# Two-layer hybrid encoder trunk: the low half of every second weight slab made by ScalarE and an adding transfer

## The chip, the core and the metric

The kernel runs on one core of a Trainium2 chip, as one program. Time is device microseconds (us) of one execution. TensorE (PE) multiplies matrices, VectorE (DVE) and ScalarE (ACT) work element by element, GpSimd (POOL) does some element work and issues some transfers, and SyncE (SP) only issues transfers between DRAM and the on-chip memory. Each engine takes its instructions strictly in the order in which they stand in its queue; engines wait for each other through semaphores.

## The reference

512 tokens with 1024 features pass through two layers. Each layer adds a normed mixer and a normed feed-forward block (FFN) to the stream x:

```python
for i in range(DEPTH):                       # two layers
    h = _rmsnorm(x, norm_g[i, 0])
    if i % 2 == 0:
        h = _ssd_mlstm_mixer(h, ...)         # one input projection, 16 SSD heads, 8 mLSTM heads, W_out
    else:
        h = _gla_mixer(h, ...)               # projections, 4 gated-linear-attention heads, W_out
    x = x + _rmsnorm(h, norm_g[i, 1])
    f = _conv_ffn(_rmsnorm(x, norm_g[i, 2]), ...)
    x = x + _rmsnorm(f, norm_g[i, 3])

def _conv_ffn(h, w_up, conv_w, conv_b, w_down):
    u = _dwconv(h @ w_up, conv_w, conv_b)
    gate, val = jnp.split(u, 2, axis=-1)
    return (jax.nn.gelu(gate, approximate=True) * val) @ w_down
```

All of it is in float32. Nearly all arithmetic is the products with the weights: 234 slabs of 128 x 1024 numbers (512 KB each), laid out in DRAM in the order in which they are used (`in_w`).

## The kernel before

**A float32 product in three faster ones.** PE multiplies the type fp32r faster than float32, but rounds its operands. So each operand is kept as two parts: `hi`, its copy rounded to fp32r, and `lo`, what the rounding took off (`lo = raw - hi`). `mm3` adds three products for each 128x128 tile of weights: hi x hi, hi x lo of the activations, and lo x hi. The `lo` slab is thus read by the third matmul of each tile.

**The weight stream.** `w_load` has SP load slab i into one of 3 `raw` buffers. `w_prep` makes the two parts: ACT copies `raw` into `hi` (the row "CAST hi<-raw"), DVE subtracts `hi` from `raw` into `lo` ("TENSOR_TENSOR lo<-raw,hi"). There are 5 buffers for `hi` and 5 for `lo` (`W_SPLIT = 5`). `w_take` prepares slabs until 4 beyond the one in use are ready (`W_AHEAD = 4`). As there are 5 buffers, the copy of slab i+4 can begin only when PE has read slab i-1 for the last time.

**Jobs.** A `Job` is one 128-row tile of W^T h: 8 tiles of weights (one slab) by 3 matmuls of 512 columns. `nat_job` takes two slabs at once and gives 256 columns with the tokens on the partitions. In the FFN the jobs follow each other one slab at a time (the down projection takes 11 tiles a job). `run_group` and `run_last` treat the tokens in two halves (RA, RB) where a norm lies between two products: the last four jobs of a block first run for RA, then for RB, so that the norm of RA can go on beside RB. There four slabs or more are held for both halves, and the next ones come late.

**The mixers.** `bal.weave` interleaves the projection jobs with the scans, in which DVE and ACT do most of the work and POOL some additions. Layer 0's mixer fills about 40 to 500 us of the trace, its output projection and norms 500 to 560, its FFN 560 to 880, the norms between the layers 880 to 960, layer 1's mixer 960 to 1140, its output projection and norms 1140 to 1200, its FFN from 1200 on.

**The order.** The program does not fix the order on an engine by its text alone: the framework's scheduler lists the instructions by its own estimates of their times, PE's too. Semaphores then hold each instruction until its operands are there.

**Slab numbers.** The trace leaves out the numbers of buffers. The slabs' `hi` and `lo` instructions stand on ACT and DVE in the order 0 to 233, so a row is assigned to its slab by counting, and PE's matmuls by their order in the built program. Layer 0's output projection runs its second half on slabs 64 to 68, layer 1's on 164 to 167; the FFN of layer 1 begins with 168 to 171, and 233 is the last slab.

Of the kernel before, what the change touches and what calls it, by code (L numbers as in the profile page):

```python
# [17 lines left out]
T = 512  # L18
D = 1024
# [10 lines left out]

# columns of the constant block
_C = {}
# [8 lines left out]
class _Balance:  # L41
    """Work issued so far to TensorE and VectorE, in ns, to weave two streams evenly."""

# [3 lines left out]
    def weave(self, streams, done):  # L47
        """streams: (generator, engine whose work it is paced by, total ns of that work, head start in ns).
        The stream least far along goes on, if what it needs is done."""
        st = [{"g": g, "e": e, "n": float(n), "t": -lead / float(n), "need": None} for g, e, n, lead in streams]  # L50
        while st:
            ok = [x for x in st if x["need"] is None or x["need"] in done]
            assert ok, [x["need"] for x in st]
            x = min(ok, key=lambda x: x["t"])
            t0 = getattr(self, x["e"])
            try:
                x["need"] = next(x["g"])
            except StopIteration:
                st.remove(x)
            x["t"] += (getattr(self, x["e"]) - t0) / x["n"]  # L60


class _Life:
    """First and last use of every work tile, in program order, and from that a slot for each."""

# [15 lines left out]
    def plan(self, slots):  # L81
        """The slot that has been free for longest."""
        until, res = [-1] * slots, []
        for a, z in zip(self.first, self.last):
            i = min(range(slots), key=lambda j: until[j])
            assert until[i] < a or until[i] < 0, "too few slots"
            until[i] = z + 1
            res.append(i)
        return res


class _Eng:
    """An engine that notes which tiles its instructions touch and how long they take."""

# [36 lines left out]
def kernel(ctx: ExitStack, tc: tile.TileContext, xin, wst, cst, dsk, gw2, out, life=None, plan=None):  # L131
# [47 lines left out]

# [1 line left out]
    cc = cp.tile([P, NCONST], F32, name="cc")  # L181
# [30 lines left out]

# [1 line left out]
    wstate = {"raw": {}, "next": 0, "ready": [], "unit": 0}  # L214
# [7 lines left out]
    def w_prep():  # L222
        i = wstate["next"]
        if i >= NSLAB:
            return
        wstate["next"] += 1
        if i not in wstate["raw"]:
            w_load(i)
        raw = wstate["raw"].pop(i)
        hi = wp.tile([P, 1024], F32R, tag="hi", name=f"hi{i}", bufs=W_SPLIT)  # L230
        lo = wp.tile([P, 1024], F32R, tag="lo", name=f"lo{i}", bufs=W_SPLIT)
        S.copy(hi, raw)
        V.tensor_tensor(lo, raw, hi, ALU.subtract)
        wstate["ready"].append((hi, lo))

    def w_take(n, width=P):
        """The next n tiles of `width` columns of the stream, as (hi, lo) pairs."""
        res = []
        for _ in range(n):
            c0 = wstate["unit"]  # L240
            i, o = divmod(c0, 1024)
            while len(wstate["ready"]) < i + 1 + W_AHEAD and wstate["next"] < NSLAB:
                w_prep()
            hi, lo = wstate["ready"][i]
            res.append((hi[:, o:o + width], lo[:, o:o + width]))
            wstate["unit"] += width
        return res

    def mm3(o, a, b, first, last):
        """o += a^T b with operands in two exact parts."""  # L250
        (ah, al), (bh, bl) = a, b
        PE.matmul(o, ah, bh, start=first, stop=False)
        PE.matmul(o, ah, bl, start=False, stop=False)
        PE.matmul(o, al, bh, start=False, stop=last)
# [4 lines left out]
    class Job:  # L259
        """One 128-row tile of W^T h."""  # L260

# [37 lines left out]
    def run_group(jobs, r, mid=None, serial=False):  # L299
        """Several jobs together, one k tile after the other (or one job after the other)."""  # L300
        if not serial:
# [42 lines left out]
    def nat_job(h, post, hi=False):  # L344
        """256 columns of h^T W with tokens on the partitions."""
        w = w_take(KD, 256)
# [12 lines left out]

# [1 line left out]
    def col_sum(o, i, acc):  # L361
        """o[tok, 2i + t]: the sum of acc[:, tok] over the partitions, for two tiles of tokens."""
        for t in range(2):
            PE.matmul(o[:, 2 * i + t:2 * i + t + 1], acc[:, t * P:(t + 1) * P], ones[:, 0:1], start=True, stop=True)

    def rstd(v, rs):
        """rs = 1 / sqrt(v / D + eps) for columns v."""
        S.activation(rs, v, AF.Sqrt, bias=eps1, scale=1.0 / D)
        V.reciprocal(rs, rs)

    def spread(o, rs):
        """o[p, tok] = rs[tok] on every partition."""
        for t in range(2):
            PE.matmul(o[:, t * P:(t + 1) * P], rs[:, t:t + 1].broadcast_to((P, P)), ident, start=True, stop=True)

    def split(xk, g, h, n, r):
        """The two exact parts of x * g (the norm's per-token factor is applied to the products)."""
        if h[n] is None:
# [5 lines left out]
    class Scale:  # L384
        """1 / rms of x for every token: as columns [tok, tile] and as a row on all partitions."""

# [28 lines left out]
    class Post:  # L415
        """x += f * g * rstd, fed with f one row tile and one token half at a time."""

# [26 lines left out]
        def finish(self, r, nxt=None):  # L444
            """nxt: (layer, which, h) of the norm that follows."""
            o = ps()
# [10 lines left out]

# [1 line left out]
    def conv(o, sc, wc, b, taps):  # L459
        """Depthwise convolution along the tokens of a PSUM tile, scaled by token, into SBUF."""  # L460
        half = taps // 2
# [54 lines left out]

# [1 line left out]
    def mixer0(h, x_again, sc, chain_of):  # L518
        done = set()
        # small block: dt and gates  # L520
        smallj = {}
# [22 lines left out]

# [1 line left out]
        rows = {}  # L546
# [11 lines left out]
        def gate_rows():  # L558
# [6 lines left out]
            V.reciprocal(d, d)  # L565
            V.tensor_tensor(u, u, d, ALU.mult)           # z = e / (2 + e)
            z2 = st()
            S.activation(z2, u, AF.Square)
            V.tensor_scalar(d, z2, 2.0 / 15, 2.0 / 13, ALU.mult, ALU.add)
            for j in range(5, -1, -1):  # L570
                V.tensor_tensor(d, d, z2, ALU.mult)
                V.tensor_scalar(d, d, 2.0 / (2 * j + 1), None, ALU.add)
            V.tensor_tensor(u, u, d, ALU.mult)           # log1p(exp(-|g|))
            lo64, hi64 = slice(0, 64), slice(64, 128)
# [32 lines left out]
            yield  # L607
            # SSD rows
            cs = st()
# [13 lines left out]
            yield  # L623
            # mLSTM rows
            ig = st()
# [30 lines left out]
            S.activation(q4[hi64], fc[hi64], AF.Exp)  # L656
            # rows to DRAM for broadcasts over the partitions
            G.dma_start(rowd[lo64], cs[lo64])
# [7 lines left out]
            G.dma_start(dskb, dsk.broadcast_to((P, 16)))  # L666
            # columns: [tok, chunk, (quantity of the pair, direction), head]
            for w, tiles in ((16, (q1, q2)), (8, (q3, q4))):
# [10 lines left out]

# [1 line left out]
        zt = [[None] * 2 for _ in range(NCH)]  # L681
# [12 lines left out]

# [1 line left out]
        def b8(ap):  # L696
# [150 lines left out]

# [1 line left out]
        kT, qT = [None] * 8, [None] * 8  # L849
# [143 lines left out]

# [1 line left out]
        part = [None] * KD  # L995
# [45 lines left out]

# [1 line left out]
    def mixer1(h, x_again, sc, chain_of):  # L1043
# [34 lines left out]
        def after(ins, first):  # L1078
            """Issue order only: groups activations by their function table."""
            tc.add_manual_dep(ins.ins, first.ins.name, mybir.DependencyInfo(  # L1080
# [58 lines left out]
        def head(hd, ps):  # L1139
# [7 lines left out]
            for dd in range(2):  # L1147
                bcv = bcs[dd][hd]
                b3 = bcv.rearrange("p (c l) -> p c l", l=64)
                ei = 63 if dd == 0 else 0  # L1150
                # first / second 64 tokens of a block in the order of the scan
                fi, se = (0, 1) if dd == 0 else (1, 0)
# [10 lines left out]
                after(S.activation(ke, ke, AF.Exp, scale=1.0 / 16.0), pin["ln"])  # L1163
                # kc: keys of the first half to its end, of the second half as they are
                kc, q2 = st(), st()
# [18 lines left out]
                yield  # L1184
                # whole-block operands of the states
                d2 = dec.rearrange("p (c u) -> p c u", u=2)
# [84 lines left out]

# [1 line left out]
    def load_x(src):  # L1273
# [8 lines left out]
    def load_first(r):  # L1282
        """Half the tokens of x, two row tiles to a tile."""
        x = [st() for _ in range(KD // 2)]
# [69 lines left out]
W_SPLIT = 5  # L1354
W_AHEAD = 4
BANKS = {"pj": 2, "ps": 3, "pm": 3}
PA = ("pj", "pm", "ps", "ps", "pm", "pj", "pm", "ps")
# [6 lines left out]
def _layout(a):  # L1364
    """Host-side layout: transposed activations, weights in the order of use, packed vectors."""
    f = lambda n: np.asarray(a[n])
# [84 lines left out]
def build(new, arrays):  # L1451
    """The program: traced once to learn how long each tile is in use, then with a slot for each."""
    plan = None
# [25 lines left out]
```

## Time and profile before

| | us |
|---|---|
| median of 3 runs | 1556.7 (1555.45 to 1556.77) |
| span of the profiled execution, first to last instruction | 1554.8 |
| what lies around the span, taken against the median | 1.9 |
| PE busy | 1508.2 (97%) |
| DVE busy | 1032.1 (66%) |
| ACT busy | 730.6 (47%) |
| POOL busy | 142.8 (9%) |

The result lists no time of its own for the profiled execution; its span is 1554.8 us, and 1.9 us is what the median of the runs lies above it. A matmul's row lasts longer than PE's step from one to the next, because matmuls are pipelined: 24 matmuls of 512 columns take 5.56 us in the FFN. The column "PEclk" is the clock that PE was granted, as a share of 2.4 GHz.

### The profile page before, as it was taken

Reading aid. Unit: us, or ns where it says so; the run is one execution under the profiler, and the core shown is the slowest. Engines: PE = TensorE matmul, PEld = TensorE weight load, DVE = VectorE, ACT = ScalarE, POOL = GpSimd, SP = SyncE. Lnnn points to the kernel's source line nnn. Section 1 sums busy time; section 2 is a strip of 40 time slices with the busy share of each in tenths; the row PEclk is TensorE's granted clock in tenths of the full one; section 3 lists DMA queues with packets and bytes.
Section 4 is the critical chain, followed back from the end, with each engine's and each line's share of the span. In section 5 each row is a group of like instructions: output and inputs, shape, how many; then the busy total and the mean of one; then the engine's idle time right before and its main releaser. Section 6 shows DMA issues by size and latency. Waiting matters only on the chain.

```text
span 1554.8 us, 22022 instructions
## 1 busy us (share of the span) xinstructions
PE 1508.2 (97%) x8616; PEld 1300.3 (84%) x8616; DVE 1032.1 (66%) x1703; ACT 730.6 (47%) x1332; POOL 142.8 (9%) x165
## 2 busy tenths in 40 slices
PE   7989999999999999999999999999999999999997
PEld 6879887888987988888888997898899888888887
DVE  6986789967754888623676378737537974267744
ACT  6445545744642664423444356436545543244432
POOL 5020321212100110000000030000003000000000
PEclk9999999999999999999999999999999999999999
DMA  5243243334322322222222132211131322222211
GB/s 186 96 156 96 82 129 102 102 114 140 131 91 79 112 86 104 95 95 95 95 95 99 69 123 103 74 56 55 65 125 69 109 95 95 95 95 95 95 69 54
DMA packets 67303, 152.46 MB, mean 98 GB/s; under 512 B 6256, under 2 KB 32896, under 8 KB 67200
## 3 DMA queue, kind: packets, MB, share of 16 engines
q1 hardware_dynamic: 61984, 145.77, 27.7%
q10 hardware_dynamic: 4752, 4.23, 0.9%
q8 instruction: 67, 1.10, 0.3%
q0 software_dynamic: 464, 1.06, 0.2%
q14 instruction: 36, 0.29, 0.1%
HBM read 146.42 MB, written 4.59 MB: 97 GB/s over the span
## 4 chain that ended last, share of the span: by engine, by line
PE 80%; DVE 11%; ACT 4%; DMA 3%; issue 2%; POOL 0%; SPq 0%; DVEq 0%; ACTq 0%; POOLq 0%
PE pj L105 31%; PE ps L105 25%; PE pm L105 24%; DVE s L105 8%; DMA s<-rowd 2%; ACT s L105 2%; DVE lo L105 2%; DVE t L105 1%; ACT hi L105 1%; ACT L105 0%; DVE pacc L105 0%; DMA raw<-in_w 0%; POOL s L105 0%; ACT msq L105 0%; DVE rd L105 0%
## 5 line engine op out<-in xcount | busy, mean ns | idle before, releaser
L105 DVE TENSOR_TENSOR lo<-raw,hi 128x1024 fp32r<-128x1024 f32 x234 | 291.4, 1249 | 220.5 <-ACT hi L105 220.3
L105 PE MATMUL pj<-s,hi 128*128 128x512 f32 (+1 forms) x1384 | 405.4, 376 | 5.2 <-ACT s L105 5.2
L105 ACT CAST hi<-raw 128x1024 fp32r<-128x1024 f32 x234 | 244.3, 1048 | 241.7 <-PE pj L105 107.7
L105 PE MATMUL pm<-s,hi 128*128 128x512 f32 (+1 forms) x1140 | 309.9, 357 | 8.4 <-ACT s L105 6.8
L105 PE MATMUL ps<-s,hi 128*128 128x512 f32 (+1 forms) x1140 | 307.3, 356 | 0.7 <-DVE t L105 0.7
L105 PEld LDWEIGHTS pj<-s,hi 128*128 128x128 f32 x1384 | 248.7, 189 | 54.6 <-ACT s L105 5.6
L105 PE MATMUL pj<-s,lo 128*128 128x512 f32 (+1 forms) x692 | 257.3, 372 | 0.0
L105 PE MATMUL pj<-hi,s 128*128 128x256 f32 x1280 | 241.6, 286 | 6.6 <-DVE s L105 3.0
L105 PEld LDWEIGHTS pm<-s,hi 128*128 128x128 f32 x1140 | 202.7, 190 | 41.6 <-ACT s L105 6.8
L105 PEld LDWEIGHTS ps<-s,hi 128*128 128x128 f32 x1140 | 202.2, 190 | 33.2 <-issue 1.1
L105 PEld LDWEIGHTS pj<-hi,s 128*128 128x128 f32 x1280 | 200.4, 189 | 9.1 <-DVE s L105 3.6
L105 PE MATMUL ps<-s,lo 128*128 128x512 f32 (+1 forms) x570 | 203.0, 356 | 1.2 <-DVE lo L105 1.2
L105 PE MATMUL pm<-s,lo 128*128 128x512 f32 (+1 forms) x570 | 203.1, 356 | 0.0
L105 PE MATMUL pj<-lo,s 128*128 128x256 f32 x640 | 180.7, 282 | 0.0
L105 DVE SCALAR_TENSOR_TENSOR s<-s,cc,s 128x511 f32<-128x511 f32 (+1 forms) x240 | 168.0, 712 | 3.2 <-ACT s L105 0.8
L105 ACT ACTIVATE s<-s 128x512 f32<-128x512 f32 (+1 forms) x145 | 90.3, 629 | 154.8 <-DVE s L105 137.0
L105 DVE TENSOR_TENSOR s<-s,s 128x512 f32<-128x512 f32 (+3 forms) x214 | 136.3, 651 | 34.0 <-ACT s L105 31.9
L105 PEld LDWEIGHTS pj<-s,lo 128*128 128x128 f32 x692 | 130.6, 189 | 23.8 <-issue 1.0
L105 ACT ACTIVATE s<-s,cc 128x512 f32<-128x512 f32 (+2 forms) x188 | 121.8, 664 | 38.2 <-DVE s L105 37.3
L105 PEld LDWEIGHTS ps<-s,lo 128*128 128x128 f32 x570 | 108.2, 190 | 17.6 <-DVE lo L105 1.6
L105 PEld LDWEIGHTS pj<-lo,s 128*128 128x128 f32 x640 | 121.5, 190 | 1.5 <-issue 1.0
L105 PEld LDWEIGHTS pm<-s,lo 128*128 128x128 f32 x570 | 108.3, 190 | 15.8
(155 smaller groups left out, 1342.5 us busy)
## 6 DMA issues: line engine op xcount, KB each, us to landing
raw<-in_w SPq DMA_DIRECT2D x234, 512.0 KB, 3.2
s<-rowd SPq DMA_DIRECT2D x64, 256.0 KB, 3.8
s<-in_x SPq DMA_DIRECT2D x8, 256.0 KB, 6.0
s<-in_x ACTq DMA_DIRECT2D x16, 128.0 KB, 2.7
xsave<-s SPq DMA_DIRECT2D x16, 128.0 KB, 2.3
s<-xsave ACTq DMA_DIRECT2D x16, 128.0 KB, 2.4
out_x<-s SPq DMA_DIRECT2D x16, 128.0 KB, 1.8
rowd<-s POOLq DMA_DIRECT2D x3, 128.0 KB, 2.3
```

The costliest lines, as they stand in the source:

```text
L105: return f(*a, **k)
```

## The change

From slab 9 on (`W_DVE = 8`), every slab with an odd number, 113 of the 234, gets its `lo` in another way: ACT writes a second rounded copy of `raw`, negated (which is -hi), into `lo`, and POOL issues a transfer that reads the same slab from DRAM once more and adds it to what stands in `lo`. DVE's subtraction goes for these slabs. The other slabs are made as before.

```diff
         S.copy(hi, raw)
-        V.tensor_tensor(lo, raw, hi, ALU.subtract)
+        if i >= W_DVE and i % 2:
+            S.activation(lo, raw, AF.Copy, scale=-1.0)
+            G.dma_start(lo, wst[i], accum_op=ALU.add)
+        else:
+            V.tensor_tensor(lo, raw, hi, ALU.subtract)
         wstate["ready"].append((hi, lo))
...
 W_AHEAD = 4
+W_DVE = 8
```

The rest of the diff takes out comments. The scheduler makes a new order from the changed program, in the mixers and at the norms; in the FFN nothing else moves. Below, rows of the built program at layer 1's output projection, with the numbers of the slabs in the names (hi165 is the rounded copy of slab 165; the number behind the underscore is the buffer's).

ACT before, at the start of that projection's second half (slabs 165 to 167; `pacc` is the first square of the norm that follows):

```order
L105 CAST hi165_10778<-raw165_10776 128x1024
L105 CAST hi166_10785<-raw166_10783 128x1024
L105 CAST hi167_10792<-raw167_10790 128x1024
L105 ACTIVATE pacc1431_10894<-pj1426_10775 128x256
L105 ACTIVATE pacc1432_10896<-pj1426_10775 128x256
```

ACT at the same place after the change:

```order
L105 CAST hi165_10856<-raw165_10854 128x1024
L105 ACTIVATE lo165_10857<-raw165_10854 128x1024
L105 CAST hi166_10864<-raw166_10862 128x1024
L105 CAST hi167_10871<-raw167_10869 128x1024
L105 ACTIVATE lo167_10872<-raw167_10869 128x1024
L105 ACTIVATE pacc1431_10974<-pj1426_10853 128x256
```

Each odd slab's negated copy stands right behind its rounded copy, and ahead of the next slab's copy and of the squares.

PE before, where slab 165 is used first:

```order
L105 MATMUL ps1445_10965<-s1254_10000,hi165_10778 128x256
L105 MATMUL ps1445_10965<-s1255_10001,hi165_10778 128x256
L105 MATMUL ps1445_10965<-s1254_10000,lo165_10779 128x256
L105 MATMUL ps1445_10965<-s1257_10009,hi165_10778 128x256
L105 MATMUL ps1445_10965<-s1258_10010,hi165_10778 128x256
```

PE at the same place after the change:

```order
L105 MATMUL ps1445_11046<-s1254_10076,hi165_10856 128x256
L105 MATMUL ps1445_11046<-s1255_10077,hi165_10856 128x256
L105 MATMUL ps1448_11082<-s1254_10076,hi166_10864 128x256
L105 MATMUL ps1448_11082<-s1255_10077,hi166_10864 128x256
L105 MATMUL ps1445_11046<-s1254_10076,lo165_10857 128x256
```

Two matmuls of slab 166 now stand ahead of the first one that reads lo165. In the same way 14 other matmuls are put ahead of the first one that reads lo171, where there were none, and 35 instead of 8 ahead of the first one that reads lo233; at lo67 nothing moves.

POOL after the change, at the same place (before, the two rows of `s1315` are followed at once by those of `accx1481`, the sum of squares of the next norm):

```order
L105 TENSOR_TENSOR s1315_10358<-s1315_10358,s1316_10359 64x4x64 x2
L105 DMA lo161_10269<-in_w 128x1024
L105 DMA lo163_10591<-in_w 128x1024
L105 DMA lo165_10857<-in_w 128x1024
L105 DMA lo167_10872<-in_w 128x1024
L105 DMA lo169_11042<-in_w 128x1024
L105 DMA lo171_11115<-in_w 128x1024
L105 TENSOR_TENSOR accx1481_11241<-accx1481_11241,t2561482_11243 128x256
```

The adding transfers stand in POOL's queue among its additions; each waits there until ACT has written its `lo`.

## Rows read from the trace of the kernel before

**Rows 1.** The page, part 1: busy time, share of the span, instructions

```profile
PE 1508.2 (97%) x8616; PEld 1300.3 (84%) x8616; DVE 1032.1 (66%) x1703; ACT 730.6 (47%) x1332; POOL 142.8 (9%) x165
```

**Rows 2.** Busy time by stretch: start:end, length, PE, PEld, DVE, ACT, POOL, PEclk

```profile
0.00:40.00 40.00, 29.47 (x203) 27.38 (x204) 27.88 (x44) 26.74 (x45) 19.55 (x42) 0.96 0.55 192
40.00:500.00 460.00, 443.43 (x2751) 386.32 (x2750) 351.10 (x643) 232.66 (x528) 79.85 (x68) 0.99 0.34 108
560.00:880.00 320.00, 320.00 (x1418) 260.75 (x1417) 195.86 (x248) 131.93 (x170) 1.19 (x3) 1.00 0.28 99
1480.00:1554.80 74.80, 64.28 (x411) 57.61 (x409) 34.39 (x72) 22.43 (x40) 0.00 (x0) 0.95 0.16 57
```

**Rows 3.** The page, part 5: the two groups that split slabs

```profile
L105 DVE TENSOR_TENSOR lo<-raw,hi 128x1024 fp32r<-128x1024 f32 x234 | 291.4, 1249 | 220.5 <-ACT hi L105 220.3
L105 ACT CAST hi<-raw 128x1024 fp32r<-128x1024 f32 x234 | 244.3, 1048 | 241.7 <-PE pj L105 107.7
```

**Rows 4.** PE in order of time: start, us, operation [idle before <- releaser]

```profile
89.33 0.73 PE L105 MATMUL pj<-s,hi 128*128 128x512 f32 x2 [3.50 <-ACT s L105]
...
111.78 0.39 PE L105 MATMUL pj<-hi,s 128*128 128x256 f32 x1 [1.15 <-DVE s L105]
...
914.98 0.61 PE L105 MATMUL ps<-ones,pacc 128*128 128x1 f32 x4 [1.31 <-DVE pacc L105]
```

**Rows 5.** Chain that ended last, 60 to 125 us, its `lo` pieces: start, us

```profile
78.86 2.27 DVE lo L105 x2
...
97.64 1.22 DVE lo L105
...
104.87 2.32 DVE lo L105
```

**Rows 6.** DVE in order of time, 907 to 913 us

```profile
910.54 1.76 DVE L105 TENSOR_TENSOR lo<-raw,hi 128x1024 fp32r<-128x1024 f32 x1
912.23 0.96 DVE L105 TENSOR_TENSOR pacc<-pacc,t 128x256 f32<-128x256 f32 x1
```

**Rows 7.** Two stretches that follow a wait of PE, columns as in rows 2

```profile
90.40:93.80 3.40, 3.40 (x10) 2.63 (x9) 2.71 (x4) 3.34 (x6) 0.94 (x2) 0.50 0.56 66
...
916.40:919.80 3.40, 3.40 (x18) 3.40 (x18) 2.59 (x8) 1.21 (x3) 0.00 (x0) 0.51 0.16 53
```

**Rows 8.** ACT in order of time in the FFN, 724 to 748 us

```profile
724.59 1.05 ACT L105 CAST hi<-raw 128x1024 fp32r<-128x1024 f32 x1 [4.05 <-PE ps L105]
...
746.83 1.06 ACT L105 CAST hi<-raw 128x1024 fp32r<-128x1024 f32 x1 [0.42 <-PE ps L105]
```

**Rows 9.** Transfers: out<-in, queue, count, KB each, us from issue to landing

```profile
raw<-in_w SPq DMA_DIRECT2D x234, 512.0 KB, 3.2
...
rowd<-s POOLq DMA_DIRECT2D x3, 128.0 KB, 2.3
...
cc<-in_c POOLq DMA_DIRECT2D x1, 229.0 KB, 5.9
```

**Rows 10.** ACT in order of time: the copies of slabs 66-68, 165-167, 171, 233

```profile
504.28 2.95 ACT L105 CAST hi<-raw 128x1024 fp32r<-128x1024 f32 x3 [7.13 <-DMA s<-in_x]
...
1141.49 2.95 ACT L105 CAST hi<-raw 128x1024 fp32r<-128x1024 f32 x3 [15.66 <-PE pj L105]
...
1164.69 1.04 ACT L105 CAST hi<-raw 128x1024 fp32r<-128x1024 f32 x1
...
1524.39 1.05 ACT L105 CAST hi<-raw 128x1024 fp32r<-128x1024 f32 x1 [0.93 <-PE pj L105]
```

**Rows 11.** PE: the first matmuls that read lo67, lo165, lo171, lo233

```profile
511.93 0.28 PE L105 MATMUL ps<-s,lo 128*128 128x256 f32 x1
...
1146.68 0.28 PE L105 MATMUL ps<-s,lo 128*128 128x256 f32 x1
...
1168.17 0.28 PE L105 MATMUL pj<-s,lo 128*128 128x256 f32 x1
...
1526.78 0.36 PE L105 MATMUL pj<-s,lo 128*128 128x256 f32 x1
```

## The prediction

> **What bounds the kernel now.** I read the page's busy times first, then busy time by stretch, then PE's waits and the chain of waits, and last the transfers and the places where a slab's `lo` is made late. PE is busy for 1508.2 of the 1554.8 us of the span [rows 1], so it waits for 46.6 us in all, and that is the most that any relief of another engine can give as long as PE's own work stays. By stretch [rows 2]: 10.5 us of it lie in the first 40 us, ahead of slab 9, the first that changes; 10.5 us lie after 1480, nearly all of it the last norm, whose chain the change does not touch; in the FFN (560 to 880 is the example, the other one reads alike) PE waits for nothing at all. So 46.6 - 10.5 - 10.5 = 25.6 us of waits remain, 16.6 of them in layer 0's mixer (460.0 - 443.43), the rest at the norms and in layer 1's mixer. The reader is to see that in the FFNs, some 40% of the time, nothing can be gained, while a slab that came late would cost there at once.
>
> **The change part by part.**
>
> *DVE.* 113 subtractions of 1249 ns each [rows 3] go: 141 us of DVE's 1032. They pay only where PE waits at the end of a chain that holds one of them. Three such waits are in the rows. The longest wait, 3.50 us at 89.33 [rows 4], has two subtractions in front of it that took 2.27 us [rows 5]; they are slabs 13 and 14, and only 13 goes: 1.1. The wait of 1.15 at 111.78 has slab 17's 1.22 in its chain (97.64; the one at 104.87 is slab 18 and stays): 1.15, all of it. The wait of 1.31 at 914.98 is for the last sum of squares, which stands on DVE right behind slab 139's subtraction of 1.76 [rows 6]: 1.3, all of it. That is 3.6 us from three waits. Of the other 19.6 us of open waits only those count that an odd slab stands in front of; others are ended by ACT, as the first in rows 4, so I take a fifth to a quarter, 4.4. Sum -8; ends 0 (the scheduler's new order brings other waits instead) and -25.6 (all go).
>
> *ACT.* 113 more copies of 1024 columns. The rounded copy of the same size takes 1048 ns [rows 3], and I take 1.05 for the negated one, 119 us in all, ACT at about 850 of 1555. ACT has the room, but it works in order: behind a negated copy stand the next slab's copy, the squares of a norm, and in the mixers the instructions that empty PE's result banks. Of the three waits in rows 4 the first is ended by ACT. The ends are 0 and 42 x 1.05 = 44 us (every one of the 42 odd slabs prepared in the two mixers, 9 to 65 and 139 to 163, delays PE by a whole copy). I take +3, three such delays, near the low end, because ACT is idle for half of that stretch (232.66 of 460 busy [rows 2]).
>
> *The new path of `lo`.* In the FFN a slab's copy starts when PE leaves a slab and its matmuls begin four jobs later: from 724.59 to the copy that starts four jobs on at 746.83 is 22.2 us [rows 8]. Of that 1.05 + 1.25 are used today. So there the whole transfer is hidden as long as it takes less than some 19 us. Here some 60 of the 113 slabs lie, and their term is nothing.
>
> The transfer itself is not in this trace. Below: 512 KB from DRAM by SP land in 3.2 us, GpSimd's 128 KB ones in 2.3 [rows 9]. It reads the slab and also what stands in `lo`, so it cannot be cheaper than the 3.2. Above: the slowest that GpSimd issues, 229 KB at the start among other transfers, took 5.9; twice that, for twice the bytes, is 11.8. The difference of 512 and 128 KB is 0.9, so a second read of 512 KB adds about 1.2 to 1.8 at the same rate; I take 5.0, near the low end, and some 0.1 for GpSimd to begin. The Trainium skill ("DMA: Bandwidth & Descriptors", "Rules for kernel authors") says that an accumulating transfer reads its destination and writes it later, and in "Anatomy of one DMA — SWDGE (gpsimd) path" gives 2.0 us plus the bytes over 436 GB/s: 3.2 for one read, which agrees with the row of SP's transfers, and as an estimate 4.4 for two. By that price the sum below would be 2.2 lower. No row here shows such a transfer.
>
> `lo` is then ready 1.05 + 0.1 + 5.0 = 6.15 us after the end of the rounded copy. Four slabs have less than that [rows 10, 11]. A slab's 24 matmuls of 512 columns take a quarter of the 22.2 us above, 5.56, so one of 256 columns, as they are here, takes 0.116.
> - Slab 67, the second of three copies from 504.28 on, ends at 506.3; lo ready 512.4; PE wants it at 511.93: 0.5.
> - Slab 165 ends at 1142.54; ready 1148.7; wanted at 1146.68, and 2 matmuls moved ahead give 0.2: 1.8.
> - Slab 171 ends at 1165.73; ready 1171.9; wanted at 1168.17, and 14 matmuls moved ahead give 1.6: 2.1.
> - Slab 233 ends at 1525.44; ready 1531.6; wanted at 1526.78, and 27 more matmuls ahead give 3.1: 1.7.
>
> Together 6.1, taken as +6. At a landing of 3.2 it is 0.3 (slab 171 alone); at 8.0 it is 3.5 + 4.8 + 5.1 + 4.7 = 18; at 11.8 it is 33. The waiting GpSimd queue matters little there: behind these transfers stand only the sums of squares of the next norm.
>
> *The clock.* After the waits at 89.33 and 914.98 the granted clock was 0.50, the lower of the two levels, for 3.4 us [rows 7], which costs half of it, 1.7. The second should go with its wait; the new wait of 2 us at slab 171 may bring another. I put 0 for both, ends -1.7 and +5.1 (three of the new waits).
>
> *Sum.* -8 + 3 + 6 + 0 = +1 on a span of 1554.8, so 1555.8; with the 1.9 around the span 1557.7, called 1558. That is 1.3 above the median of 1556.7, within 0.2% (3.1 us, about what a measurement of this kernel can tell from no change).
>
> **The rivals.**
>
> *DVE's relief wins: faster.* The transfer lands in 3.2 to 4 (new waits 0.3 to 2.5), ACT's copies fit into its idle time (0 to +1), and DVE's shorter queue also shortens waits that the chain puts down to ACT, since ACT stands waiting for DVE through the mixers. -8 to -10, and one drop of the clock less: 1548 to 1553, at best 1545. For it: DVE is busy for 351 of 460 us in layer 0's mixer, the busiest engine beside PE [rows 2]. Against it: each wait has more than one cause, and the order there is a new one.
>
> *The adding transfer is slow: slower.* One mechanism, at slabs 67, 165, 171 and 233, where PE stands in order before a matmul that reads `lo`. The price is the lateness of the four, 10 us at a landing of 6.0 and 18 at 8.0, with up to 5 us of lower clock behind it; against -5 from the other terms. It decides from a landing of about 5.5 on (each us more is worth four) and gives 1562 at 6.0, 1570 to 1575 at 8.0. For it: the same engines must read two streams and add, and GpSimd's only transfer of this order took 5.9. Against it: that one ran among the loads of the start.
>
> *ACT in order: slower.* The negated copies stand in front of the instructions that empty PE's banks or feed its next product, ten of the 42 in the mixers instead of three: +10 instead of +3, 1565. For it: the wait at 89.33 was ended by ACT. Against: the subtraction that goes was just as long, and stood on an engine that is fuller.
>
> *The shift does not reach PE at all* (waits and new path both hidden): 1556.7. It has the same answer as the forecast and is counted with it.
>
> **How the numbers follow.** No change (the forecast and the last case) 0.32, 1553.6 to 1559.8. Faster by over 0.2%: 0.31. Slower: 0.37, of it the slow transfer 0.27 and ACT in order 0.10. As both signs have much of the chance, the likeliest case's own range is 1554 to 1560, while the range given, 1549 to 1572, takes in most of the first rival and the second up to a landing of 8; beyond each end I leave a tenth.
>
> **What would show it.** Right: a group of about 113 ScalarE copies `lo<-raw` near 1.05 us; DVE near 890 us busy; the adding transfers landing in 4 to 6 us; PE busy within a few us of 1508; new waits of PE for a transfer at slabs 165, 171 and 233 alone, each under 3 us; the wait before the sum of squares at 914.98 gone or shorter; nothing new in the FFN. Wrong: landings over 8 us, waits for `lo` in the FFN, waits of PE for ACT in the mixers that add up to over 10 us, or PE's open waits cut by half.

## The result, and the profile after

The changed kernel takes 1594.6 us (median of 4 runs, 1591.9 to 1597.1) against 1556.1 for the kernel before beside it: a ratio of 1.025, interval 1.0235 to 1.0264. It is 38 us slower, far outside the range given. The profiled execution took 1594.3 us, its span is 1592.6: 37.8 more than before.

Page, part 1, after (columns as in [rows 1]):

```profile
PE 1522.4 (96%) x8616; PEld 1311.4 (82%) x8616; DVE 899.8 (57%) x1590; ACT 832.7 (52%) x1445; POOL 237.8 (15%) x278
```

VectorE has lost 132 us of work and ScalarE has gained 102, much as intended. PE does the same 8616 matmuls, but its busy time has grown by 14.2 us, and its waits from 46.6 to 1592.6 - 1522.4 = 70.2, by 23.6. The sum is the 37.8.

Busy time by stretch, after (columns as in [rows 2]; the stretches hold about what 40:500, 560:880, 1140:1200, 1200:1480 and 1480 to the end held before):

```profile
40.00:514.50 474.50, 448.59 (x2741) 391.08 (x2740) 316.00 (x612) 256.97 (x555) 102.98 (x97) 0.97 0.53 137
574.30:894.30 320.00, 320.00 (x1418) 260.74 (x1417) 162.60 (x219) 158.62 (x200) 26.62 (x33) 1.00 0.60 148
1155.00:1233.70 78.70, 68.13 (x474) 64.83 (x473) 34.24 (x72) 41.25 (x84) 17.11 (x20) 0.91 0.37 93
1233.70:1513.70 280.00, 278.15 (x1203) 225.36 (x1202) 147.41 (x198) 138.78 (x171) 21.81 (x25) 1.00 0.60 149
1513.70:1592.60 78.90, 65.13 (x412) 58.12 (x410) 29.71 (x68) 26.14 (x44) 3.49 (x4) 0.94 0.32 80
```

Before, for the two of these stretches that [rows 2] doesn't have:

```profile
1140.00:1200.00 60.00, 58.12 (x448) 56.49 (x447) 40.36 (x77) 34.28 (x76) 11.93 (x14) 0.97 0.24 82
1200.00:1480.00 280.00, 280.00 (x1215) 227.23 (x1214) 177.91 (x223) 117.51 (x148) 0.00 (x0) 1.00 0.28 99
```

Set against [rows 2], the stretch of layer 0's mixer is 14.5 us longer, that of the output projection and norms of layer 1 18.7 longer (60.0 to 78.7), and the end 4.1. The limits don't fall on quite the same matmuls (474 lie in the 78.7 us, 448 in the 60.0 before). By PE's first use of a slab, which marks the same place before and after, 13.9 us are lost up to slab 65, the last of layer 0's mixer, 3.8 from there to slab 163, which takes in the norms between the layers, 16.2 from 163 to 174, which are layer 1's output projection and norms, and 3.9 behind slab 174, at the very end. In the feed-forward blocks nothing is lost: from slab 75 to 132 and from 174 to 233 PE takes what it took, to 0.1 us, though the share of the DMA engines has doubled there (0.28 to 0.60). The 1.85 us by which PE falls short of 280.00 in the second of them are a wait for lo173 at its start. The loss thus has two kinds of place, and they have different causes.

*A late `lo`, at the norms and output projections.* Page, parts 3, 5 and 6, after: packets, MB and share of the DMA engines of GpSimd's queue; GpSimd's issues and ScalarE's negated copies as in [rows 3]; the transfers as in [rows 9]:

```profile
q0 software_dynamic: 16736, 60.32, 22.0%
...
L105 POOL DMA_DIRECT2D lo<-in_w x113 | 99.4, 880 | 999.6 <-ACT lo L105 871.6
...
L105 ACT ACTIVATE lo<-raw 128x1024 fp32r<-128x1024 f32 x113 | 119.2, 1055 | 10.7 <-PE pj L105 10.7
...
raw<-in_w SPq DMA_DIRECT2D x234, 512.0 KB, 3.8
lo<-in_w POOLq DMA_DIRECT2D x113, 512.0 KB, 7.9
s<-rowd SPq DMA_DIRECT2D x64, 256.0 KB, 4.2
...
xsave<-s SPq DMA_DIRECT2D x16, 128.0 KB, 3.6
```

And the row transfers before:

```profile
s<-rowd SPq DMA_DIRECT2D x64, 256.0 KB, 3.8
```

The adding transfer lands in 7.9 us, 2.5 times the 3.2 of a plain load of the same slab by SP [rows 9]. Transfers that run beside it got slower: slab loads 3.2 to 3.8, the row transfers of layer 0's mixer 3.8 to 4.2, the stores of x 2.3 to 3.6. PE's waits after, by what ended them (us in total, times, longest):

```profile
PE pm L105 <- ACT mst_c L105: 11.5, 4, 4.5
PE ps L105 <- DMA lo<-in_w: 10.8, 5, 5.3
PE pj L105 <- DMA lo<-in_w: 7.1, 3, 4.0
```

With one of 0.4 that is not shown, PE stands 18.3 us before a matmul that reads a `lo` still under way. PE in order of time, after, at the first matmul that reads lo165 and the first that reads lo171 (before: [rows 11], no wait):

```profile
1171.08 0.58 PE L105 MATMUL ps<-s,lo 128*128 128x256 f32 x1 [5.26 <-DMA lo<-in_w]
...
1201.33 0.58 PE L105 MATMUL pj<-s,lo 128*128 128x256 f32 x1 [4.03 <-DMA lo<-in_w]
```

Behind such a wait PE also runs slower. Four stretches after, columns as in [rows 2]:

```profile
374.30:381.10 6.80, 5.18 (x21) 5.02 (x22) 4.34 (x12) 4.01 (x12) 0.00 (x0) 0.50 0.38 117
...
958.00:968.20 10.20, 10.20 (x25) 5.80 (x23) 5.51 (x9) 2.59 (x5) 0.00 (x0) 0.50 0.32 74
1169.60:1176.40 6.80, 5.32 (x25) 5.32 (x26) 1.56 (x2) 1.77 (x4) 0.00 (x0) 0.50 0.88 268
1200.40:1207.20 6.80, 5.87 (x27) 5.87 (x28) 2.38 (x4) 2.25 (x6) 3.91 (x5) 0.50 0.27 80
```

The granted clock is 0.50, the lower level, for 6.8 us around or after the waits of 4.54, 5.26 and 4.03; after the shorter waits of before it was 3.4 [rows 7]. Ahead of the last drop, at the very end, the low stretches add up to 51 us after and 17 before. PE is busy for 45.2 us of the 51 and for 17.0 of the 17; half of the 28.3 us more is 14.1, and that is the 14.2 us of extra busy time. Not all of it is the price of a wait: in the longest stretch, 10.2 us from 958.0 on, PE is busy throughout and hasn't waited for more than 0.3 us in the 33 us before. The plain transfer of e2 below has a stretch as long there (948.0) with no late `lo` near it, and the kernel before has none there. Why the clock falls there stays open.

*Late rows, in layer 0's mixer.* PE never waits for a `lo` there. PE's waits for `mst_c` by ScalarE before, to set against the 11.5 above:

```profile
PE pm L105 <- ACT mst_c L105: 4.6, 4, 2.1
```

Chain of waits at one of the four places where PE waits for `mst_c`, after (start, us, what):

```profile
363.84 7.85 DMA s<-rowd
371.69 0.02 issue
371.71 1.92 ACT s L105 x7
...
374.16 0.93 ACT hi L105
375.10 0.53 ACT s L105
375.63 0.16 ACT mst_c L105
```

The same place before:

```profile
358.53 4.44 DMA s<-rowd
...
363.34 1.13 DVE lo L105
...
365.81 0.26 ACT mst_c L105
```

GpSimd after, in order of time, and PE at the end of this chain, after and before:

```profile
363.82 0.88 POOL L105 DMA_DIRECT2D lo<-in_w  x1
...
375.92 0.77 PE L105 MATMUL pm<-mst_c,s 128*128 128x129 f32 x2 [4.54 <-ACT mst_c L105]
...
366.21 0.46 PE L105 MATMUL pm<-mst_c,s 128*128 128x129 f32 x2 [0.75 <-ACT mst_c L105]
```

A row transfer (`s<-rowd`: SP spreads some rows of the mixer's gates over the partitions) was issued at 363.84, just as GpSimd issued an adding transfer at 363.82, and took 7.85 us instead of 4.44. ScalarE then makes `mst_c`, for which PE waits 4.54 us here and waited 0.75 at the same place before. The subtraction that stood in this chain is gone, but the row in front of it took 3.4 us longer.

### The profile page after: what moved, and what is told of

It is laid out like the page before. It is cut to its first block, busy times and chain, and to the rows that moved or that the text cites. A ratio compares the mean times of both kernels' runs of the same rounds, so it can differ in the third digit from the quotient of the medians.

```text
span 1592.6 us, 22276 instructions
## 1 busy us (share of the span) xinstructions
PE 1522.4 (96%) x8616; PEld 1311.4 (82%) x8616; DVE 899.8 (57%) x1590; ACT 832.7 (52%) x1445; POOL 237.8 (15%) x278
## 3 DMA queue, kind: packets, MB, share of 16 engines
q0 software_dynamic: 16736, 60.32, 22.0%
## 4 chain that ended last, share of the span: by engine, by line
PE 63%; issue 16%; DVE 8%; DMA 7%; ACT 4%; POOL 1%; SPq 0%; POOLq 0%; DVEq 0%; ACTq 0%
PE pj L105 27%; PE ps L105 19%; PE pm L105 17%; DVE s L105 7%; DMA s<-rowd 4%; DMA lo<-in_w 3%; ACT s L105 2%; POOL lo L105 1%; DVE t L105 1%; ACT hi L105 1%; POOL s L105 0%; ACT lo L105 0%; ACT L105 0%; DMA s<-in_x 0%; ACT t L105 0%
## 5 line engine op out<-in xcount | busy, mean ns | idle before, releaser
L105 DVE TENSOR_TENSOR lo<-raw,hi 128x1024 fp32r<-128x1024 f32 x121 | 149.3, 1234 | 219.8 <-ACT hi L105 219.6
L105 PE MATMUL pj<-hi,s 128*128 128x256 f32 x1280 | 245.6, 289 | 8.4 <-ACT s L105 5.8
L105 POOL DMA_DIRECT2D lo<-in_w x113 | 99.4, 880 | 999.6 <-ACT lo L105 871.6
L105 PE MATMUL ps<-s,lo 128*128 128x512 f32 (+1 forms) x570 | 204.2, 359 | 12.1 <-DMA lo<-in_w 10.8
L105 PEld LDWEIGHTS pj<-hi,s 128*128 128x128 f32 x1280 | 203.7, 192 | 11.4 <-ACT s L105 6.7
L105 DVE TENSOR_TENSOR s<-s,s 128x512 f32<-128x512 f32 (+3 forms) x214 | 139.6, 668 | 38.3 <-ACT s L105 36.3
L105 PEld LDWEIGHTS ps<-s,lo 128*128 128x128 f32 x570 | 108.8, 191 | 29.6 <-DMA lo<-in_w 12.1
L105 ACT ACTIVATE lo<-raw 128x1024 fp32r<-128x1024 f32 x113 | 119.2, 1055 | 10.7 <-PE pj L105 10.7
```

The lines of the kernel that those rows point to most:

```text
L105: return f(*a, **k)
```

## The experiments

The theory: the loss has two parts, (a) PE waits at the norms and output projections for a `lo` that lands after 7.9 us, with the lower clock behind, and (b) in layer 0's mixer the adding transfers make the row transfers late, on which the chain stands. The rivals: ScalarE's copies in order, the scheduler's new order, GpSimd's queue, or a cost that each transfer has wherever it is. Diffs are against the changed kernel unless said. "Mixer" is how much later than before (506.0 us) PE first used slab 65, the last of the mixer; "rows" the median landing of a row transfer; "lo" PE's waits for `lo` from a transfer. The last four columns come from one profiled execution of each run. In e3, e4 and e11 nothing in the mixer was changed, and there the column "mixer" reads -1.0, +1.8 and +0.3: so much comes and goes from run to run.

| run | ratio to before, interval | span against 1554.8 | mixer | rows | lo |
|---|---|---|---|---|---|
| the change | 1.025 (1.0235-1.0264) | +37.8 | +13.9 | 4.2 | 18.3 |
| e1 no transfer | 1.0009 (0.9994-1.0024) | -0.2 | +2.0 | 3.6 | 0 |
| e2 plain transfer | 1.0091 (1.0063-1.0119) | +10.8 | +5.8 | 3.9 | 3.6 |
| e3 not in mixer 0 | 1.0196 (1.0149-1.0243) | +22.1 | -1.0 | 3.9 | 19.6 |
| e4 FFN only | 1.0014 (1.0003-1.0025) | +3.2 | +1.8 | 3.8 | 0 |
| e5 an eighth | 1.0043 (1.0026-1.0059) | +4.9 | +3.9 | 3.7 | 2.5 |
| e6 traffic only | 1.0111 (1.0093-1.013) | +16.1 | +11.8 | 4.6 | 0 |
| e7 not the tight slabs | 1.0065 (1.0045-1.0084) | +7.9 | +11.8 | 4.5 | 0 |
| e8 relief alone | 1.0024 (1.0014-1.0035) | +2.5 | +5.5 | 3.7 | 0 |
| e9 no rows, no tight | 0.9992 (0.9976-1.0009) | -3.3 | -0.4 | 3.9 | 0 |
| e10 rows only | 1.01 (1.0085-1.0114) | +15.0 | +14.7 | 4.4 | 0 |
| e11 slab 139 | 0.9992 (0.9982-1.0001) | -2.2 | +0.3 | 3.8 | 0 |
| e12 rows twice | 1.0252 (1.0235-1.0268) | +38.6 | +39.3 | 4.4 | 0 |

**e1, no transfer.**

```diff
             S.activation(lo, raw, AF.Copy, scale=-1.0)
-            G.dma_start(lo, wst[i], accum_op=ALU.add)
```

> The odd slabs from 9 on keep ScalarE's negated copy and lose the adding transfer, so their lo holds only -hi (the part that the transfer adds is left out). Theory 'transfers': the 37.8 us come from the adding transfers, 18 to 25 us from PE standing before a lo that lands late (slabs 67, 137, 163 to 173, 233), with the clock drops behind it, and about 14 us from layer 0's mixer, where the transfers lengthen SP's row transfers (median 3.8 us before, 4.9 when one of them overlaps a lo transfer). Without them both go and VectorE's relief is left: 1546 to 1557. Rival 'ScalarE in order': the 14 us of the mixer come from 28 negated copies and the scheduler's new order, so they stay while the late lo goes: 1566 to 1572, with PE's waits for ACT's mst_c still near 11 us.

1.0009: nothing is left of the loss. All 113 subtractions are gone and all 113 copies are in place, in nearly the changed kernel's order (of PE's 2680 matmuls ahead of slab 65, 2656 stand where they stand after the change, against 1938 for the kernel before), and the mixer is 2.0 us late instead of 13.9. So the copies and the order are not the cause. PE's wait for `mst_c` in this run:

```profile
PE pm L105 <- ACT mst_c L105: 5.9, 4, 2.8
```

It was 4.6 before and 11.5 after. The run lies at the upper end of the 1546 to 1557 that the theory gave; the gain that these numbers allowed isn't there (e8).

**e2, a plain transfer.**

```diff
-            G.dma_start(lo, wst[i], accum_op=ALU.add)
+            G.dma_start(lo, wst[i])
```

> The transfer of the odd slabs overwrites instead of adding, so their lo holds raw, not raw - hi. Theory 'the addition is what is slow': 512 KB land in 3.3 to 4.5 us as SP's do (3.2 before), the late lo shrinks to under 3 us in sum, the row transfers stay near 4.0 us and the time is 1550 to 1560. Rival 'any second stream through GpSimd's queue': landing stays at 6 to 8 us and the time at 1585 or more. Between them, with a landing of about 5 us, my forecast's own sum would hold: about 1558 if the mixer is unharmed, 1570 if it isn't.

Page, parts 3 and 6:

```profile
q0 software_dynamic: 16736, 60.32, 11.3%
...
lo<-in_w POOLq DMA_DIRECT2D x113, 512.0 KB, 4.4
s<-rowd SPq DMA_DIRECT2D x64, 256.0 KB, 3.9
```

The same bytes in as many packets, with every matmul in the changed kernel's order, but 11.3% of the DMA engines' time instead of 22.0%, 4.4 us instead of 7.9, 3.6 us of waits for `lo` instead of 18.3, and the mixer +5.8. Most of the price is the addition, as the first theory said, with the landing at its upper end; a second plain stream still costs 0.9%. With 1568.3 this is the third case: my forecast's sum, with a harmed mixer.

**e3, not in layer 0's mixer.**

```diff
-        if i >= W_DVE and i % 2:
+        if i >= 66 and i % 2:
```

> The change only from slab 67 on; layer 0's mixer is as before. If its share of the loss is the mixer's own (whatever the cause), the mixer ends where it did (about 14 us earlier than after the change) and the rest stays: 1578 to 1583. Rival 'one common cause spread over the run': 84 of 113 transfers stay and with them 84/113 of 38 us: 1584 or more, with PE's waits spread as evenly.

The mixer ends where it did (-1.0), the rest stays. PE's waits:

```profile
PE ps L105 <- DMA lo<-in_w: 12.9, 5, 3.6
PE pj L105 <- DMA lo<-in_w: 6.4, 3, 4.1
```

The median of its four runs is 1584.4 with a wide interval, on the border of the two cases, so the time doesn't tell them apart. The trace does: 19.6 us of waits stand at the output projections, the norms and the end, as after the change.

**e4, the feed-forward blocks only.**

```diff
-        if i >= W_DVE and i % 2:
+        if (75 <= i < 132 or 177 <= i < 230) and i % 2:
```

> The change only for the odd slabs 75 to 131 and 177 to 229, 56 of the 113, in the steady part of both feed-forward blocks, where lo has some 12 us to spare. Theory 'what counts is where PE or a chain waits': nothing shows, 1554 to 1558. Rival 'each transfer costs by its traffic or by the clock': 56/113 of 38 us, 1575. Rival 'DVE's relief is worth something wherever': under 1550.

1.0014, with an interval up to 1.0025: 56 transfers of 7.9 us each, and PE never waits for one. Of the +3.2 of span, 1.8 had been lost in the mixer, where nothing was changed. A cost that each transfer has wherever it is (1575) is excluded.

**e5, an eighth of the bytes.**

```diff
-            G.dma_start(lo, wst[i], accum_op=ALU.add)
+            G.dma_start(lo[:, 0:128], wst[i][:, 0:128], accum_op=ALU.add)
```

> As the change, but each adding transfer moves only 128 of the slab's 1024 columns (64 KB; the other columns of lo keep -hi). GpSimd issues as many transfers, in the same places of its queue. Theory 'traffic in layer 0's mixer': the row transfers come as before, the mixer ends within 3 us of before, lo lands in about 3 us, 1555 to 1560. Rival 'GpSimd's queue': its additions stand behind the transfers that wait for ScalarE, so the mixer still ends 12 us or more late and the time is 1568 or more.

Page, parts 3, 5 and 6:

```profile
q0 software_dynamic: 16736, 8.48, 4.2%
...
L105 POOL DMA_DIRECT2D lo<-in_w x113 | 99.3, 879 | 998.8 <-ACT lo L105 884.7
...
s<-rowd SPq DMA_DIRECT2D x64, 256.0 KB, 3.7
lo<-in_w POOLq DMA_DIRECT2D x113, 64.0 KB, 3.5
```

GpSimd issues as many transfers in the same 99.3 us and waits as long for ScalarE, yet the mixer is 3.9 us late and not 13.9. The rival "GpSimd's queue" falls; what counts is the bytes. The mixer is 0.9 beyond the 3 us that I had allowed, and the time 1.7 beyond the 1560.

**e6, the traffic without the dependence** (against the kernel before; 61 instead of 64 work tiles make room):

```diff
+            junk = junks[i // 2 % 2]
+            G.tensor_copy(junk[:, 0:1], hi[:, 0:1])
+            G.dma_start(junk, wst[i][:, :896], accum_op=ALU.add)
             V.tensor_tensor(lo, raw, hi, ALU.subtract)
```

> The kernel before with all its subtractions, and beside each odd slab from 9 on an adding transfer of 448 KB into a tile that nobody reads (two such tiles; 61 instead of 64 work tiles make room; a copy of one column of hi by GpSimd, 128 x 1, sets when each starts). Theory 'traffic': layer 0's mixer ends 8 to 16 us late, PE never waits for lo from a transfer, nothing else is lost: 1563 to 1574. Rival 'the loss in the mixer comes from lo itself being late or from the new order': 1555 to 1559.

Page, part 6:

```profile
junka<-in_w POOLq DMA_DIRECT2D x57, 448.0 KB, 7.1
...
s<-rowd SPq DMA_DIRECT2D x64, 256.0 KB, 4.6
```

1572.5: all subtractions are there, nobody reads what the transfers bring, the order is nearly that of before, and the mixer is still 11.8 us late. So the traffic costs it without any dependence of PE on what is brought. Two things came with this edit, and their share was not measured: GpSimd's 113 small copies (353.2 us busy instead of 142.8, the transfers' issues with them) and the three work tiles less. Another 4.3 of the run's 16.1 us are lost behind the mixer, against the "nothing else is lost" of the expectation.

**e7, without the ten tight slabs.**

```diff
+TIGHT = (67, 71, 137, 163, 165, 167, 169, 171, 173, 233)
-        if i >= W_DVE and i % 2:
+        if i >= W_DVE and i % 2 and i not in TIGHT:
```

> The change without the ten slabs whose lo has little time (67, 71, 137, 163, 165, 167, 169, 171, 173, 233), which VectorE makes as before. If the two losses are separate and add up, the late lo's 18 to 22 us go and the mixer's 14 us stay: 1568 to 1573. Rival 'the lateness moves on to the neighbours' or 'the traffic costs at the norms too': 1576 or more.

PE waits for no `lo` from a transfer, and the mixer's loss stays, +11.8. The time, 1565.1, is under the case, since 5 us come back between slabs 137 and 141, as in e9 below, and the neighbours aren't late either. The two losses are separate: the spans of e3 and e10 add up to 22.1 + 15.0 = 37.1, the change's is 37.8.

**e8, the relief alone.**

```diff
-            S.activation(lo, raw, AF.Copy, scale=-1.0)
-            G.dma_start(lo, wst[i], accum_op=ALU.add)
+            lo = hi
```

> VectorE's 113 subtractions go and nothing takes their place: lo of an odd slab is the hi tile itself (its subtraction is left out). This is the relief term by itself, which my forecast put at -8 (0 to -25.6): 1545 to 1549. The run without transfers, at 1.0009 of before, makes me doubt it: either relief and ScalarE's copies cancel (relief -8, copies +8: this run near 1548), or both are near nothing (this run 1553 to 1557).

1.0024: with VectorE at 900.4 us busy instead of 1032.1, and nothing in exchange, the kernel is 3.5 us slower, past both cases. The mixer is 5.5 late, and 3.1 come back by slab 174. In total the relief is worth nothing here. But this run has an order of its own: of the 2680 matmuls ahead of slab 65, 2091 stand where they stood before and 1887 where they stand after the change. So it doesn't show the relief at an unchanged order, and why the mixer gets longer (the scheduler's order, or more drops of the clock in it: 23.8 us of lower clock in the mixer against 6.8 before) stays open.

**e9, no rows and no tight slabs:** 78 of the 113.

```diff
-        if i >= W_DVE and i % 2:
+        if i >= 59 and i % 2 and i not in TIGHT:
```

> The change for 78 of the 113 slabs: from slab 59 on, whose transfers start after the last row transfer of layer 0's mixer, without the ten tight slabs. If the loss is made of these two places only, nothing is left of it: 1553 to 1558, ratio 0.998 to 1.002. Rival 'the traffic also costs at the norms and in layer 1's mixer': 1562 or more. If VectorE's relief is worth anything in layer 1's mixer and at the norms, it shows here as 1548 to 1553.

0.9992, interval 0.9976 to 1.0009: nothing of the loss is left. PE at the wait of 1.31 us of [rows 4]:

```profile
914.92 0.61 PE L105 MATMUL ps<-ones,pacc 128*128 128x1 f32 x4 [0.50 <-DVE pacc L105]
```

The span is 3.3 shorter, all of it won between slabs 137 and 141, but the interval doesn't tell it from no change.

**e10, only beside the rows:** the 25 odd slabs 9 to 57.

```diff
-        if i >= W_DVE and i % 2:
+        if W_DVE <= i < 59 and i % 2:
```

> The complement inside layer 0's mixer: the change only for the 25 odd slabs 9 to 57, whose transfers run beside the row transfers. If the loss there comes from the row transfers that the chain waits for, it is all here: the mixer ends 10 to 14 us late and the time is 1566 to 1571. Rival 'the last part of the mixer and the output projection carry it': under 1561.

1.0100, and the mixer +14.7: the whole of the mixer's loss. From the single transfers in the trace: 39 rows that overlapped an adding transfer landed in 5.04 us (median, longest 9.98), the other 25 in 3.70 (longest 4.79). PE's wait:

```profile
PE pm L105 <- ACT mst_c L105: 10.4, 4, 4.0
```

**e11, one slab.**

```diff
-        if i >= W_DVE and i % 2:
+        if i == 139:
```

> The change for one slab, 139, whose subtraction of 1.76 us stood on VectorE ahead of the last sums of squares of the norm between the layers. In the run that spared rows and tight slabs PE came out of that place 4.4 us early. If VectorE's relief at this one slab does that: the wait before the sum of squares falls from 1.31 to about 0.5 us, the clock's drop behind it goes, 1551 to 1554. Rival 'it was the other slabs or chance of the clock': 1555 to 1558.

1554.25, ratio 0.9992 up to 1.0001. A miss on the mechanism: the wait before the sum of squares is 1.14 and not 0.5, so the other slabs of e9 had a share in it; the clock didn't drop behind it. A gain can't be told from none.

**e12, each row twice** (against the kernel before; the transfers to `r4`, `w` and `qs` alike):

```diff
                 SY.dma_start(w, rowd[64 + row:65 + row, :].broadcast_to((P, T)))
+                SY.dma_start(w, rowd[64 + row:65 + row, :].broadcast_to((P, T)))
```

> The kernel before, no adding transfers; each of the 64 row transfers of layer 0's mixer is issued twice into the same tile, the second behind the first, so the rows land some 3.8 us later. If the mixer stands on the arrival of the rows, lateness alone must cost it: the adding transfers made 39 of 64 rows about 1.3 us later and cost 14.8 us, so here with 3.8 us for each of 64 the mixer ends at least 20 and up to 80 us late: 1576 to 1640. If the rows were not what it waits for: under 1563.

PE's waits, and the page, part 6:

```profile
PE pm L105 <- ACT mst_c L105: 14.8, 3, 8.6
```

```profile
s<-rowd SPq DMA_DIRECT2D x128, 256.0 KB, 4.4
```

The second transfer of a pair landed 4.0 us behind the first (median). Without any adding transfer, rows that land late cost the mixer 39.3 us, in good part through the same wait for `mst_c`. That the mixer stands on its rows is shown by this, and that the transfers make the rows late by e6 and e10; whether the rows lose that time in the DMA engines or in the memory behind them, no run separates. The second issue also holds up SP's slab loads behind it, so the 39.3 is no exact price of a microsecond.

## Why the prediction was wrong, step by step

*"I take 5.0, near the low end"* is the first step that failed. The landing was 7.9, inside the bounds that I had (3.2 and 11.8), and I had reasoned that the second read would cost only at the rate of its bytes (1.2 to 1.8 us). e2 shows what the addition does: at equal bytes it doubles the engines' time (11.3% to 22.0%) and adds 3.5 us to the landing. The Trainium skill's sentence ("DMA: Bandwidth & Descriptors", "Rules for kernel authors"), that an accumulating transfer reads its destination and writes it later, agrees in kind. The 4.4 that I estimated for two reads from the same page's "Anatomy of one DMA — SWDGE (gpsimd) path" is what the plain transfer takes here, and the adding one takes 7.9, so the measurement decides against the estimate.

The term measured 18.3 us where the sum had +6. My own price at 8.0 was 18, but that agreement is partly luck: slabs 67, 165, 171 and 233 waited 0.60, 5.26, 4.03 and 2.17, 12.1 in all, and the other 6.3 stood at slabs 71, 137, 163, 169 and 173, which "Four slabs have less than that" passed over. Before the change they had 6.6 to 10.2 us from the end of the rounded copy to PE's first read of `lo`, more than the 6.15 of the forecast; after it their `lo` landed 6.7 to 10.1 us behind that copy, later than PE wanted it.

*The clock, "I put 0".* PE's busy time grew by 14.2 us for the same matmuls, nearly three times the upper end of 5.1. I counted a drop of 3.4 us, as in [rows 7], for three waits; waits of 4 to 5 us were followed by 6.8, and the longest drop, 10.2 us, followed no wait at all.

*The sum had no term for what the transfers do to other transfers.* This is the step that was missing, and 14 us of the result: I priced the new path only where PE reads `lo`, and in the mixer there are 16 us and more to spare for that. I asked what stands behind the transfers in GpSimd's queue (rightly nothing, e5), not what shares the DMA engines with them. The profile had the hint: rows of 3.8 us that a chain waits for. The Trainium skill ("DMA: Bandwidth & Descriptors", "Queues, rings and completion order") says that each DMA engine takes turns between the queues that have work for it, packet by packet; that is a rule that spoke against the change, and e10 agrees with it: 3.70 us alone, 5.04 beside an adding transfer.

*VectorE, -8.* Nothing of it is to be seen in the total: 1.0009 with ScalarE's copies, 1.0024 alone. Of the three waits named, the one of 1.15 at 111.78 is gone after the change, and so is the one before the sum of squares at 914.98 (0.50 in e9), but a wait of 2.16 for lo137 stands near it instead; the longest, 3.50 at 89.33, for which I credited 1.1, has one as long in its place (3.8, 3 us earlier, before another matmul). In e1 PE is 3.5 us ahead at slab 20, and 1.5 behind at slab 34: what VectorE gave early in the mixer was gone some 120 us later. The open waits of PE in a mixer are the ends of chains through several engines and transfers, and 132 us less of VectorE's work didn't shorten those.

*ScalarE, +3.* Right in price (113 x 1055 ns = 119.2; the busy time grew by 102, as rows that follow each other closely overlap, three copies taking 2.95 us in [rows 10]). The effect on PE isn't separated from the new order: e1, with the copies, isn't slower than e8 without, but their orders differ. The rival "ACT in order", which gave 1565, falls by e1.

*The feed-forward blocks, nothing.* Right, and shown alone by e4.

*The rival "the adding transfer is slow"* had the right side and the right mechanism for half of the loss. At a landing of 8.0 it gave 1570 to 1575; e3, which is that case nearly by itself, measured 1584 with a span of 1576.9.

## What to carry to other kernels

A transfer that is hidden from the engine that reads its data is not yet free: ask which short transfers run beside it and whether a chain waits for their landing. Price an unseen kind of transfer from its upper bound where a few late places decide, and count every place whose time to spare lies under that bound. Add lower clock behind a new long wait of PE: here 3.4 to 6.8 us followed each of the six waits of 3.6 us and more that the changed kernel has after 40 us. Work taken from an engine that is not the bound bought nothing here in total, though two of the three waits that it was to relieve did go: name what the time won there will meet next.

## What the runs showed of the hardware that I had not expected

- The addition in a transfer doubled the DMA engines' time for the same 60.32 MB (22.0% of the span against 11.3%), and the issue on GpSimd took 880 ns whatever the size (512 or 64 KB), against 542 for the plain transfer.
- Landing of an adding transfer: 3.5 us for 64 KB, 7.1 for 448, 7.9 for 512; a plain one of 512 KB took 4.4 by GpSimd and 3.2 by SP.
- A row transfer of 256 KB took longer by itself (3.8) than a slab of 512 KB (3.2), and up to 9.98 beside an adding transfer.
- The lower clock lasted 6.8 us at waits of 4.03, 4.54 and 5.26 us, and 3.4 after those of 1.31 and 3.50; in e1 it lasted 6.8 at one of 3.6, and in e7 3.4 at one of 4.08, so the size of the wait alone doesn't set it. After the change it also fell for 10.2 us with PE busy throughout. With no long wait added it came and went from run to run: behind slab 139's wait it was there before and missing in e11 at nearly the same wait (1.14 against 1.31).
